# Hybrid attention / HGRN2 / mixture-of-experts layer on one core: two small loads moved to ScalarE's DMA queue, and unread products on TensorE around the first row transposes

## The chip, the cores and the metric

One core of a Trainium2 chip runs the whole layer as one program. The metric is the device time of one execution in microseconds (us), as the median of several runs. TensorE is called PE below, VectorE DVE, ScalarE ACT, GpSimd POOL and SyncE SP, as in the profile.

## What is computed

The reference is one layer over 16 meta tokens and 1024 tokens of width 1024. Cut to what matters here:

```python
h = concatenate([zeros, meta_tokens, x])              # rows of width 1024
a = rmsnorm(h, g_mix)                                 # x * rsqrt(mean(x^2) + eps) * g_mix
proj = a @ w_in                                       # 1024 -> 3584
# stick-breaking attention on 8 heads of 64, HGRN2 recurrence on 4 heads of 128,
# the latter with lower bounds lb = softmax(lb_logits) for its forget gate
h = h + mixed @ w_out
m = rmsnorm(h, g_ffn)
h = h + hierarchical_moe(m)                           # 4 groups x 8 experts, 2 experts per token
out = rmsnorm(h, g_final)
```

The change touches only the way from `x`, `meta_tokens`, `g_mix` and `lb_logits` to the first columns of `proj`.

## The kernel before, in words

**Stages.** The input rows are normed, transposed and split into a high and a low part (`aH`, `aL`, 1040 columns of tokens). Then four rounds follow, in each of which projections, the HGRN2 recurrence and stick-breaking attention run interleaved by `merge`; then the output projection and the router (up to about 750 us), then the 32 experts (up to about 1337 us), then the last norm. Every projection is three products per 128 rows of the contraction (`whi*aH`, `whi*aL`, `wlo*aH`, lines 203 to 205).

**The head of the program.** `head_project` for head 0 (lines 518 to 549) does the input norm as it goes. `load_rows(i)` (line 143) loads row block `i`: block -1 is the 16 meta tokens, blocks 0 to 7 are 128 tokens each; below they are called block -1, block 0 and so on. `norm_rows(i)` (lines 146 to 162) squares a block on ACT with a sum (line 152), makes the factor on DVE (line 100) and POOL (line 101), multiplies block, factor and `gm` on DVE into `xn` (line 154), transposes `xn` on PE in two halves of four (line 158), copies each half to `aH` on ACT (line 160) and subtracts on DVE into `aL` (line 161). `gm` is `g_mix` spread over the 128 partitions; its load stands between those of blocks 0 and 1 on SP's queue (line 519). `load_block` (line 189) loads a block of `w_in` into `wraw`, and `split_block(nc.gpsimd)` splits it on ACT (`whi`, line 195) and POOL (`wlo`, line 197); the first two blocks are the forget columns and the input columns of head 0. The blocks -1, 0 and 1 are normed first, then the two weight blocks are split, then block 2 is normed, then `project_chunk` makes the first 272 columns (`START[0]`: blocks -1, 0 and 1) of the forget projection, and so on alternately.

**The small load.** `lbt` holds `lb_logits` on 8 partitions. It is loaded on SP's queue at line 458, transposed at line 460, copied on DVE at line 462, and used in the evacuation of the forget projection (`ev_f`, lines 500 and 501). At line 529 the same load stands a second time.

**Order.** Each engine runs its instructions in the order in which the framework's scheduler placed them when the program was built; it places an instruction of an engine when its inputs are ready by the scheduler's own estimate, the earlier in the program text first. Instructions of different engines wait for each other by semaphores. The PSUM tag `tr` has two buffers, so the third transpose group waits for the DVE subtraction that reads the first.

**The unread products.** `warm(n)` (lines 815 to 822) multiplies the identity by itself `n` times into a PSUM bank of tag `o` that nobody reads, each product placed behind the one before. Before the change it is used only at the end of the router stage.

Of the kernel before, what the change touches and what calls it, by code (L numbers as in the profile page):

```python
# [18 lines left out]
P = 128  # L19
# [4 lines left out]
D = 1024  # L24
# [4 lines left out]
def bcast(ap, n):  # L29
    return bass.AP(tensor=ap.tensor, offset=ap.offset, ap=[[0, P], [1, n]])  # L30
# [3 lines left out]
def kernel(  # L34
# [21 lines left out]
    nc = tc.nc  # L56
# [14 lines left out]
    def behind(first, then):  # L71

        tc.add_manual_dep(then.ins, first.ins.name, mybir.DependencyInfo(mybir.DependencyClass.NoSync, mybir.DependencyReason.SCHED_ONLY), reason="order")

    def bank(tag):
        return psum.tile([P, 512], F32, name=tag, tag=tag)

    def bank4(tag):
        return bank(tag).rearrange("p (a b) -> p a b", b=P)


    ones = const.tile([P, P], F32, name="ones")
    nc.vector.memset(ones, 1.0)
# [5 lines left out]
    nc.vector.memset(small[:, 1:17], -0.5)  # L89
    zero, mhalf = small[:, 0:1], small[:, 1:17]  # L90
    nc.scalar.activation(small[:, 17:18], zero, AF.Sigmoid)

    def mixed_rows(i, n):

# [41 lines left out]

    gm = att.tile([P, NT + 1, 4, 64], F32, name="gm", tag="av", bufs=1).rearrange("p a b c -> p (a b c)")[:, :D]

    def load_rows(i):

        n = M if i < 0 else P
        xt = att.tile([P, W], F32, name="xt", tag=("beta1", "keep")[i % 2], bufs=2)[:n, :D]
        nc.sync.dma_start(xt, meta_tokens if i < 0 else x2[P * i:P * i + P])
        return xt

    def norm_rows(i, xt):

        n = M if i < 0 else P
        c0 = 0 if i < 0 else M + P * i
        ss = att.tile([P, 1], F32, name="xss")[:n]  # L150
        xn = att.tile([P, W], F32, name="xn", tag=("kh", "kl")[i % 2])[:n, :D]
        nc.scalar.activation(xn, xt, AF.Square, accum_out=ss)
        r = rstd_of(att, ss, 1, D, "rx")[:n]
        nc.vector.scalar_tensor_tensor(xn, xt, r, gm[:n], op0=ALU.mult, op1=ALU.mult)
        for h in range(2):
            pt = bank4("tr")
            for k in range(4):
                nc.tensor.transpose(pt[:, k, :n], xn[:, (4 * h + k) * P:(4 * h + k + 1) * P], ident[:n, :n])
            hi = aH[:, 4 * h:4 * h + 4, c0:c0 + n]
            nc.scalar.activation(hi, pt[:, :, :n], AF.Copy)  # L160
            done = nc.vector.tensor_sub(aL[:, 4 * h:4 * h + 4, c0:c0 + n], pt[:, :, :n], hi.bitcast(F32))  # L161
        return done

    def merge(*streams, until=None):

# [289 lines left out]


    lbt = mc.tile([8, P], F32, name="lbt")
    nc.sync.dma_start(lbt, lb_logits.rearrange("l (h d) -> (l h) d", d=P))
    lbp = bank("tr")
    nc.tensor.transpose(lbp[:, :8], lbt, ident[:8, :8])  # L460
    lbs = mc.tile([P, 4, 4], F32, name="lbs")
# [31 lines left out]
    def head_project(hd, Q2, F, kR, V):  # L493
# [19 lines left out]
        if hd > 0:  # L513
            yield from project(1536 + P * hd, REAL, ev_q)
            yield from project(2048 + P * hd, FULL, ev_f)
            yield from project(2560 + P * hd, FULL, ev_i)
        else:
            xs = {i: load_rows(i) for i in (-1, 0)}
            nc.sync.dma_start(gm, bcast(g_mix, D))
            for i in (1, 2):  # L520
                xs[i] = load_rows(i)
                load_block()
            for i in (-1, 0, 1):
                norm_rows(i, xs.pop(i))
                xs[i + 4] = load_rows(i + 4)
            split_block(nc.gpsimd)
            split_block(nc.gpsimd)
            (_, fh, fl), (_, ih, il) = halves.pop(0), halves.pop(0)
            nc.sync.dma_start(lbt, lb_logits.rearrange("l (h d) -> (l h) d", d=P))
            norm_rows(2, xs.pop(2))  # L530
            xs[6] = load_rows(6)
            yield from project_chunk(fh, fl, *START[0], ev_f)
            norm_rows(3, xs.pop(3))
            xs[7] = load_rows(7)
            yield from project_chunk(ih, il, *START[0], ev_i)
            norm_rows(4, xs.pop(4))
            load_block()
            yield from project_chunk(fh, fl, *START[1], ev_f)
            norm_rows(5, xs.pop(5))
            norm_rows(6, xs.pop(6))  # L540
            yield from project_chunk(ih, il, *START[1], ev_i)
            last = norm_rows(7, xs.pop(7))
            make_masks(last)
            nc.sync.dma_start(sbg, bcast(sb_gain, 512))
            nc.sync.dma_start(hgg, bcast(hg_gain, 512))
            yield from project_chunk(fh, fl, *START[2], ev_f)
            split_block()
            yield from project_chunk(ih, il, *START[2], ev_i)
            yield from project(1536, REAL, ev_q)
# [260 lines left out]
    def load_until(n):  # L810
        while len(pieces) < min(n, 6 * NE):
            e, part = divmod(len(pieces), 6)
            pieces.append(load_piece(slice(e, e + 1), part, len(pieces)))

    def warm(n, first=None):

        w = bank("o")[:, :P]
        for _ in range(n):
            mm = nc.tensor.matmul(w, lhsT=ident, rhs=ident, start=True, stop=True)
            if first is not None:  # L820
                behind(first, mm)
            first = mm

    def route(i, rp, r):

# [275 lines left out]
    turned = []  # L1101
# [244 lines left out]
```

## Time and profile before

| | us |
|---|---|
| median of 3 runs | 1359.17 |
| lowest and highest of the 3 | 1356.43 and 1359.87 |
| profiled execution, its own time | 1358.34 |
| its span, from first to last instruction | 1356.7 |
| PE busy | 1279.8 (94% of the span) |
| DVE busy | 1064.8 (78%) |
| ACT busy | 840.9 (62%) |
| POOL busy | 292.7 (22%) |

The rows further below come from the profiled execution. A row of the timeline has the start and the duration in us, the engine, the line, the operation, output and inputs with their shapes, how many instructions are merged into the row, and in square brackets the idle time of the engine before it and what ended that. SPq is SP's DMA queue: the duration is that of issuing, not of the transfer. [...] In the first stretch of the trace the granted clock is recorded as 1.00 throughout, also where the products take as long as at 0.50 elsewhere; there the durations are read.

### The profile page before, as it was taken

To read this page: it belongs to the slowest core of one execution; us is meant where nothing else is said; L and a number is where in the kernel's file an instruction comes from. 1 tells how busy PE (TensorE), PEld (TensorE's weight loads), DVE (VectorE), ACT (ScalarE), POOL (GpSimd) and SP (SyncE) were. 2 spreads that over 40 slices of the span, in tenths; PEclk is the share of its full clock that TensorE was granted. 3 is DMA by queue.
4 is the path that set the end of the run, shared out by engine and by line. 5 is a ranking of instruction groups with operands and counts; after the bars stand their busy time and mean duration, and the time that the engine had idled before them with its cause. 6 is when DMAs were issued, how large, how long until landed. Compare 5 with 4: busy or idle time off the path is not lost.

```text
span 1356.7 us, 19397 instructions
## 1 busy us (share of the span) xinstructions
PE 1279.8 (94%) x6872; PEld 1001.8 (74%) x6873; DVE 1064.8 (78%) x1677; ACT 840.9 (62%) x1374; POOL 292.7 (22%) x373
## 2 busy tenths in 40 slices
PE   6999889998999899999999999999999999999993
PEld 5888788877888788777888666666666666666661
DVE  5384887478756877699667888888898898898885
ACT  5333654266334643555223888888888888888884
POOL 3202340034103420252111111111111111111114
PEclk9999999999999999999999999999999999999996
DMA  6111001110011010175587699999999999999916
GB/s 204 46 33 47 21 24 36 39 44 20 24 31 48 24 36 21 53 239 176 198 297 254 233 400 406 398 376 409 361 374 399 361 402 374 371 407 366 359 40 264
DMA packets 84307, 278.65 MB, mean 205 GB/s; under 512 B 12806, under 2 KB 45598, under 8 KB 59632
## 3 DMA queue, kind: packets, MB, share of 16 engines
q1 hardware_dynamic: 70048, 243.53, 46.8%
q0 software_dynamic: 14016, 33.33, 8.3%
q8 instruction: 55, 0.90, 0.3%
q10 hardware_dynamic: 144, 0.52, 0.1%
q14 instruction: 44, 0.36, 0.1%
HBM read 258.59 MB, written 35.52 MB: 217 GB/s over the span
## 4 chain that ended last, share of the span: by engine, by line
issue 38%; PE 31%; DVE 11%; POOL 9%; DMA 6%; ACT 3%; POOLq 0%; SPq 0%; ACTq 0%; DVEq 0%
PE pj L205 6%; PE pj L204 6%; PE pj L203 5%; DVE keep L331 4%; POOL out_dram L1139 3%; POOL xg L1086 3%; DMA mrows<-mt 3%; DVE beta L336 2%; DMA out_dram<-y,idx 2%; PE o L382 2%; PE pj L776 1%; PE z L608 1%; POOL keep L323 1%; PE pj L775 1%; PE tr L355 1%
## 5 line engine op out<-in xcount | busy, mean ns | idle before, releaser
L1124 DVE TENSOR_TENSOR wl<-w,wh 128x1024 fp32r<-128x1024 f32 x384 | 457.1, 1220 | 62.2 <-ACT wh L1118 60.7
L1118 ACT ACTIVATE wh<-w 128x1024 fp32r<-128x1024 f32 x384 | 402.4, 1057 | 73.1 <-PE pj L1148 22.6
L203 PE MATMUL pj<-aH,whi 128*128 128x346 f32 (+4 forms) x576 | 208.8, 363 | 0.9 <-ACT aH L160 0.5
L204 PE MATMUL pj<-aL,whi 128*128 128x346 f32 (+4 forms) x576 | 203.1, 353 | 1.1 <-DVE aL L161 1.0
L205 PE MATMUL pj<-aH,wlo 128*128 128x346 f32 (+4 forms) x576 | 202.4, 351 | 0.0
L203 PEld LDWEIGHTS pj<-aH,whi 128*128 128x128 f32 x576 | 110.2, 192 | 8.2 <-ACT aH L160 1.2
L204 PEld LDWEIGHTS pj<-aL,whi 128*128 128x128 f32 x576 | 110.0, 191 | 7.7 <-DVE aL L161 1.7
L205 PEld LDWEIGHTS pj<-aH,wlo 128*128 128x128 f32 x576 | 109.9, 191 | 7.3
L1086 POOL DMA_INDIRECT xg<-mrows,idx x32 | 44.3, 1384 | 293.5 <-PE tr L1095 286.8
L1147 PE MATMUL o<-wl,hH 128*96 128x512 f32 x256 | 104.3, 407 | 0.8 <-DVE wl L1124 0.8
L1147 PE MATMUL pj<-wl,emH 128*96 128x512 f32 x256 | 103.9, 406 | 0.2 <-DVE wl L1124 0.2
L1146 PE MATMUL pj<-wh,emH 128*96 128x512 f32 x256 | 103.7, 405 | 0.3 <-ACT emH L1108 0.3
L1146 PE MATMUL o<-wh,hH 128*96 128x512 f32 x256 | 102.0, 398 | 1.7 <-ACT hH L1194 1.7
L1146 PE MATMUL z<-wh,emH 128*96 128x512 f32 x256 | 103.0, 402 | 0.0
L331 DVE TENSOR_TENSOR_SCAN keep<-keep,small 128x144 f32<-128x144 f32 (+3 forms) x64 | 90.9, 1421 | 12.9 <-POOL keep L323 12.1
L1148 PE MATMUL o<-wh,hL 128*96 128x512 f32 x256 | 101.0, 395 | 0.0
L1147 PE MATMUL z<-wl,emH 128*96 128x512 f32 x256 | 101.0, 394 | 0.0
L1148 PE MATMUL pj<-wh,emL 128*96 128x512 f32 x256 | 100.5, 393 | 0.4 <-DVE emL L1109 0.4
L1148 PE MATMUL z<-wh,emL 128*96 128x512 f32 x256 | 100.2, 392 | 0.0
L1139 POOL DMA_INDIRECT out_dram<-y,idx x31 | 49.1, 1583 | 183.5 <-ACT y L1204 183.5
L358 ACT ACTIVATE wH<-tr 128x512 fp32r<-128x512 f32 (+1 forms) x80 | 44.6, 558 | 56.6 <-PE tr L355 55.9
L195 ACT ACTIVATE whi<-wraw 128x1024 fp32r<-128x1024 f32 x28 | 29.6, 1058 | 74.9 <-PE pj L204 52.6
(285 smaller groups left out, 2586.4 us busy)
## 6 DMA issues: line engine op xcount, KB each, us to landing
w<-in_w_expert_gate_dram SPq DMA_DIRECT2D x64, 1024.0 KB, 8.5
w<-in_w_expert_up_dram SPq DMA_DIRECT2D x64, 1024.0 KB, 8.8
w<-in_w_expert_down_dram SPq DMA_DIRECT2D x64, 1024.0 KB, 7.9
wraw<-in_w_in_dram SPq DMA_DIRECT2D x28, 512.0 KB, 3.9
out_dram<-ht POOLq DMA_DIRECT2D x11, 512.0 KB, 3.7
xt<-in_x_dram SPq DMA_DIRECT2D x8, 512.0 KB, 4.6
wraw<-in_w_out_dram SPq DMA_DIRECT2D x8, 512.0 KB, 5.3
mxt<-mixed SPq DMA_DIRECT2D x16, 256.0 KB, 4.7
```

What stands on the lines that cost most here:

```text
L203: nc.tensor.matmul(ps[:, :n], lhsT=hi[:, k], rhs=aH[:, k, c0:c0 + n], start=k == 0, stop=False)
L204: nc.tensor.matmul(ps[:, :n], lhsT=hi[:, k], rhs=aL[:, k, c0:c0 + n], start=False, stop=False)
L205: nc.tensor.matmul(ps[:, :n], lhsT=lo[:, k], rhs=aH[:, k, c0:c0 + n], start=False, stop=k == KD - 1)
L331: nc.vector.tensor_tensor_scan(kr, kr, zero.to_broadcast([P, S]), 1.0, op0=ALU.mult, op1=ALU.add)
L358: nc.scalar.activation(hi[:, :n], pt[:, :n], AF.Copy)
L1086: nc.gpsimd.indirect_dma_start(out=dst, out_offset=None, in_=src, in_offset=bass.IndirectOffsetOnAxis(ap=ix, axis=0), bounds_check=T - 1, ...
L1118: nc.scalar.activation(wh, w, AF.Copy)
L1124: nc.vector.tensor_sub(wl, w, wh.bitcast(F32))
L1139: nc.gpsimd.indirect_dma_start(out=out2, out_offset=bass.IndirectOffsetOnAxis(ap=ix, axis=0), in_=y, in_offset=None, bounds_check=T - 1, o ...
L1146: nc.tensor.matmul(ps, lhsT=hi, rhs=wh[:, u], start=k + u == 0, stop=False)
L1147: nc.tensor.matmul(ps, lhsT=hi, rhs=wl[:, u], start=False, stop=False)
L1148: nc.tensor.matmul(ps, lhsT=lo, rhs=wh[:, u], start=False, stop=k + u == last)
```

## The change

`warm` is defined at the top of the kernel instead of before `route`. Twenty unread products stand right after the identity is made. The loads of `gm` and of `lbt` are issued from ACT's queue: that of `gm` where the tile is allocated, ahead of every row load in the text, and that of `lbt` at its old place in the text. The load of `gm` between the row loads is gone, and so is the second load of `lbt`. `norm_rows` can return its last transpose instead of its last subtraction, and two unread products are placed behind the last transpose of the blocks -1, 0, 1 and 2. The unread products are fp32, 128x128 by 128x128.

```diff
+    def warm(n, first=None):
+        w = bank("o")[:, :P]
+        for _ in range(n):
+            mm = nc.tensor.matmul(w, lhsT=ident, rhs=ident, start=True, stop=True)
+            if first is not None:
+                behind(first, mm)
+            first = mm
...
     nc.scalar.activation(small[:, 17:18], zero, AF.Sigmoid)
+
+    warm(20)
...
     gm = att.tile([P, NT + 1, 4, 64], F32, name="gm", tag="av", bufs=1).rearrange("p a b c -> p (a b c)")[:, :D]
+    nc.scalar.dma_start(gm, bcast(g_mix, D))
...
-    def norm_rows(i, xt):
+    def norm_rows(i, xt, turned=False):
...
-                nc.tensor.transpose(pt[:, k, :n], xn[:, (4 * h + k) * P:(4 * h + k + 1) * P], ident[:n, :n])
+                mm = nc.tensor.transpose(pt[:, k, :n], xn[:, (4 * h + k) * P:(4 * h + k + 1) * P], ident[:n, :n])
...
-        return done
+        return mm if turned else done
...
-    nc.sync.dma_start(lbt, lb_logits.rearrange("l (h d) -> (l h) d", d=P))
+    nc.scalar.dma_start(lbt, lb_logits.rearrange("l (h d) -> (l h) d", d=P))
...
             xs = {i: load_rows(i) for i in (-1, 0)}
-            nc.sync.dma_start(gm, bcast(g_mix, D))
...
             for i in (-1, 0, 1):
-                norm_rows(i, xs.pop(i))
+                warm(2, norm_rows(i, xs.pop(i), True))
                 xs[i + 4] = load_rows(i + 4)
...
-            nc.sync.dma_start(lbt, lb_logits.rearrange("l (h d) -> (l h) d", d=P))
-            norm_rows(2, xs.pop(2))
+            warm(2, norm_rows(2, xs.pop(2), True))
...
-    def warm(n, first=None):
```

## Rows read from the trace of the kernel before

**Rows 1.** The windows view of the expert stage: length, then busy time and instructions of PE, PE's weight loads, DVE, ACT and POOL, granted clock, DMA share, GB/s.

```profile
760.00:1320.00 560.00, 559.79 (x2615) 383.01 (x2614) 500.29 (x498) 470.94 (x560) 89.62 (x61) 1.00 0.93 361
```

**Rows 2.** The chain of work that ended last, in order of time, cut to the first 32 us (start us, us, what).

```profile
3.07 7.72 DMA wraw<-in_w_in_dram
10.81 1.07 ACT whi L195
11.95 2.75 POOL wlo L197
...
15.16 0.55 POOL rx L101
...
15.74 1.15 DVE xn L154
```

**Rows 3.** The timeline of the first 30 us, SP's queue alone: issues of loads.

```profile
0.83 0.40 SPq L458 DMA_DIRECT2D lbt<-in_lb_logits_dram  x1
1.29 0.33 SPq L143 DMA_DIRECT2D xt<-in_meta_tokens_dram  x1
...
2.12 0.43 SPq L519 DMA_DIRECT2D gm<-in_g_mix_dram  x1
2.59 0.43 SPq L143 DMA_DIRECT2D xt<-in_x_dram  x1
3.07 0.57 SPq L189 DMA_DIRECT2D wraw<-in_w_in_dram  x1
```

**Rows 4.** The windows view of the first 8 us in steps of 1 us, two of them; the last number is GB/s.

```profile
3.00:4.00 1.00, 0.00 (x0) 0.00 (x0) 0.00 (x0) 0.66 (x1) 0.00 (x0) 1.00 0.78 205
...
7.00:8.00 1.00, 0.00 (x0) 0.00 (x0) 0.30 (x3) 0.00 (x0) 0.57 (x1) 1.00 0.99 395
```

**Rows 5.** The timeline of all engines, 0 to 32 us: the identity, ACT's first work, the small load's transpose and copy, block 0's factor, block -1's and block 3's `xn`, and the second `wlo`.

```profile
0.83 1.28 ACT L91 ACT_TABLE_LOAD   x1 [0.70 <-PEq L1332]
...
1.17 0.34 POOL L85 TENSOR_SCALAR_AFFINE_SELECT ident<-ones 128x128 f32<-128x128 f32 x1
...
2.39 0.24 PE L460 MATMUL tr<-ident,lbt 8*128 8x8 f32 x1 [2.39 <-DMA lbt<-in_lb_logits_dram]
...
6.92 0.15 DVE L100 TENSOR_SCALAR rx<-xss 128x1 f32<-128x1 f32 x1 [2.26 <-ACT xn L152]
6.99 0.16 DVE L462 COPY lbs<-tr 128x8 f32<-128x8 f32 x1
...
7.84 1.27 DVE L154 SCALAR_TENSOR_TENSOR xn<-xt,rx,gm 16x1024 f32<-16x1024 f32 x1 [0.69 <-POOL rx L101]
...
16.41 2.85 POOL L197 TENSOR_TENSOR wlo<-wraw,whi 128x1024 fp32r<-128x1024 f32 x1 [0.70 <-ACT whi L195]
...
19.79 1.29 DVE L154 SCALAR_TENSOR_TENSOR xn<-xt,rx,gm 128x1024 f32<-128x1024 f32 x1 [1.50 <-POOL rx L101]
```

**Rows 6.** The timeline of PE alone, 9 to 24 us: transposes of blocks -1, 0 and 2, then the products of the forget projection's first chunk. From 18.45 to 21.72 eleven products are listed, from 22.22 to 23.35 ten.

```profile
9.17 1.03 PE L158 MATMUL tr<-ident,xn 16*128 16x16 f32 x8 [6.54 <-DVE xn L154]
10.82 1.97 PE L158 MATMUL tr<-ident,xn 128*128 128x128 f32 x8 [0.62 <-DVE aL L161]
...
17.68 1.12 PE L158 MATMUL tr<-ident,xn 128*128 128x128 f32 x4 [0.70 <-DVE aL L161]
18.45 0.57 PE L204 MATMUL pj<-aL,whi 128*128 128x272 f32 x1
...
19.05 1.05 PE L158 MATMUL tr<-ident,xn 128*128 128x128 f32 x4
...
20.36 0.43 PE L205 MATMUL pj<-aH,wlo 128*128 128x272 f32 x1
...
21.72 0.40 PE L205 MATMUL pj<-aH,wlo 128*128 128x272 f32 x1
...
22.22 0.29 PE L205 MATMUL pj<-aH,wlo 128*128 128x272 f32 x1
...
23.35 0.29 PE L205 MATMUL pj<-aH,wlo 128*128 128x272 f32 x1
```

**Rows 7.** The timeline of all engines, 23 to 31 us: block 3's transposes, the `xn` of blocks 5 and 6, and the first product of the second chunk that reads `aL`.

```profile
23.48 1.04 PE L158 MATMUL tr<-ident,xn 128*128 128x128 f32 x8
...
26.96 2.48 DVE L154 SCALAR_TENSOR_TENSOR xn<-xt,rx,gm 128x1024 f32<-128x1024 f32 x2 [0.40 <-POOL rx L101]
...
30.10 0.44 PE L204 MATMUL pj<-aL,whi 128*128 128x384 f32 x1 [0.95 <-DVE aL L161]
```

**Rows 8.** The timeline of PE, 746 to 753 us: the fourteen unread products of the old `warm(14)`, as 28 instructions.

```profile
749.77 3.37 PE L819 MATMUL o<-ident 128*128 128x128 f32 x28
```

**Rows 9.** The windows view in steps of 10 us, the three stretches between 60 and 740 us in which the granted clock (third number from the end) is not 1.00.

```profile
190.00:200.00 10.00, 8.24 (x48) 8.04 (x48) 9.59 (x20) 2.36 (x6) 4.12 (x4) 0.83 0.00 0
...
480.00:490.00 10.00, 8.12 (x55) 7.39 (x53) 9.72 (x12) 5.83 (x15) 2.63 (x5) 0.98 0.16 46
490.00:500.00 10.00, 10.00 (x64) 9.51 (x64) 6.33 (x18) 3.78 (x8) 2.22 (x2) 0.85 0.05 15
```

**Rows 10.** The windows view in steps of 1 us: before the first of these falls, and around 1329 us.

```profile
194.00:195.00 1.00, 0.00 (x0) 0.00 (x0) 1.00 (x3) 0.00 (x0) 0.00 (x0) 1.00 0.00 0
...
1327.00:1328.00 1.00, 0.48 (x4) 0.30 (x4) 1.00 (x1) 0.37 (x1) 0.00 (x0) 1.00 1.09 414
...
1330.00:1331.00 1.00, 1.00 (x3) 0.56 (x3) 1.00 (x1) 0.45 (x3) 0.72 (x1) 0.50 1.07 336
```

More of the change, by code (lines that the diff above doesn't have):

```diff
@@ L813, in load_until @@
             pieces.append(load_piece(slice(e, e + 1), part, len(pieces)))
-    def warm(n, first=None):
[L817 to L822, printed above, removed]
     def route(i, rp, r):
```

## The prediction, as put on record

> **What bounds the kernel now.** I read the page first, then the windows, then the chain of waits of the first 32 us, and last the timeline of the engines there. The profiled execution took 1358.34 us for a span of 1356.7. Nearly all of that is TensorE: in the expert stage PE is busy 559.79 of 560 us [rows 1]. Nothing downstream runs against an outside clock, so what the head of the program gives up moves the rest earlier by as much. The change can therefore be read in the first 30 us.
>
> There the chain of waits goes through the first weight block, not through the norm: the load of `wraw` is issued at 3.07 and lands 7.72 us later, ACT splits it at 10.81, POOL makes `wlo` until about 15.1, and only then does POOL come to block 2's factor at 15.16 and DVE to its `xn` at 15.74 [rows 2]. The rows of block -1 have their own earlier wait, `xn` at 7.84 [rows 5], but this one doesn't end last. From 17.68 on PE has work without pause: block 2's transposes, then the first chunk of the forget projection [rows 6]. The reader should see two speeds in rows 6: products of 272 columns follow each other every (21.72 - 20.36) / 6 = 0.227 us, and from about 21.9 on every (23.35 - 22.22) / 9 = 0.126 us. [...] The same pair shows in eight transposes: 1.97 us slow [rows 6], 1.04 fast [rows 7]. So the head pays twice: it waits for a weight block, and then does its first dense work at the low clock.
>
> **The change part by part.**
>
> *Loads moved off SP's queue.* The issues of `lbt` (0.83 to 1.29) and `gm` (2.12 to 2.59) leave the queue ahead of `wraw`'s [rows 3]: 0.46 + 0.47 = 0.93 us less before it is issued. The bytes ahead of it are the same, `gm`'s included, so the landing gains between 0 (if the engines that move bytes are the limit) and 0.93. They moved 205 GB/s from 3 to 4 us and 395 from 7 to 8 [rows 4], so the early part isn't full; I take 0.8. The split on ACT and POOL, block 2's factor and its `xn` move with it. The second `lbt` load stood on SP's queue behind three row loads, where nothing waited for it: 0. ACT issues the two loads instead; at SP's prices [rows 3] that is 0.9 us, ahead of its table load [rows 5] or behind it. At worst the squares of the first block start 0.9 later, which isn't on the chain either: 0. An earlier `gm` brings block -1's `xn` forward by at most 0.7 us (DVE is free from 7.15, starts at 7.84 [rows 5]), which isn't on the chain: 0.
>
> *Twenty unread products.* Fourteen show as 28 instructions in 3.37 us, (3.37 - 0.28) / 27 = 0.115 us each [rows 8], fast. Slow, I take the spacing of slow transposes, (1.97 - 0.43) / 7 = 0.22 [rows 6]. Forty instructions from about 1.55, when the identity is there [rows 5], end at 1.55 + 4.6 = 6.2 if all were fast and 1.55 + 8.8 = 10.4 if all were slow. I assume that the clock is low at first and rises on the way, as it did during the eleven products of rows 6, and take the middle, about 8.2. PE's next real job came at 9.17 [rows 6]: hidden. One wait is new: `lbt`'s transpose (line 460, at 2.39 before) now sits behind the twenty, and DVE's copy of it (line 462) stands in DVE's order right before block -1's `xn` [rows 5]. By 8.2 + 0.24 + 0.2 that `xn` would start at about 8.6 instead of 7.84, 0.8 late; blocks -1 and 0 get 0.9 + 0.4 back from faster transposes: 0, if the clock is up.
>
> *Two products behind each of four blocks.* Four instructions, 0.46 us fast, 0.88 slow. Behind blocks -1, 0 and 1 PE waits anyway (0.62 before block 0's transposes [rows 6], and longer once these are faster): 0. Behind block 2 PE is dense: +0.46.
>
> *The clock.* If it is still high at the first dense work, block 2's transposes take 1.04 instead of 1.12 + 1.05 = 2.17 (1.13 less), and eleven slow products [rows 6] save 11 x (0.227 - 0.126) = 1.1.
>
> *Sum.* -0.8 - 1.13 - 1.1 + 0.46 = -2.6 us at block 3's transposes (23.48 before). Are these ready then? They need block 3's `xn`, done at 19.79 + 1.29 = 21.08 [rows 5], which hangs on the second `wlo` on POOL (16.41 + 2.85) and moves with the weight loads: 20.3, against the 20.9 that PE then reaches. So that is late next, and it caps the gain at about 3.3. Behind it the way from 23.48 to the second chunk's product at 30.10 [rows 7] runs over DVE, with PE waiting 0.95 us, and moves as a whole.
>
> *What the trace does not price.* A shift of everything by 2 or 3 us changes where PE's pauses fall. PE stood still from 194 to 195 us [rows 10], and the granted clock fell after it: a mean of 0.83 over 10 us is 0.17 x 10 / 0.5 = 3.4 us at half rate, a loss of about 1.7 us; two rounds later it fell once more, by 0.02 + 0.15 [rows 9]. One such fall may come or go: -1.7 to +1.7, taken as 0, since as much speaks for either sign. The runs shown lie 3.44 us apart.
>
> **The rivals.**
>
> *The clock is low again at the first dense work.* Between the twenty products and the first chunk PE does transposes with pauses, and only six unread products. For it: from 9.17 to 17.68 PE ran mostly transposes, and those of block 2 were as slow as those of block 0 [rows 6]; near 1327 four transposes between two pauses weren't enough, and the next products ran at 0.50 [rows 10]. Against it: the pauses here would be near 1 us, shorter than the full stop at 194. Then the two clock terms vanish, the products behind block 2 cost 0.88, and -0.8 + 0.88 leaves about 1358.4: no change. [...]
>
> *More than the sum.* If the first chunk's products no longer alternate with block 2's transposes, the cap of 3.3 is reached, and with one fall of the clock avoided 1358.34 - 3.3 - 1.7 = 1353.3.
>
> *Slower: the new wait on DVE.* If the clock doesn't rise during the twenty products, they end at 10.4; `lbt`'s transpose and copy end at 10.8, and block -1's `xn` starts at 10.9, 3.1 us late, with block 0's and block 1's in DVE's order behind it. With 0.88 for the slow products behind block 2 that is 1358.34 + 4.0 = 1362.3. It decides from the point where the twenty end later than about 7.84 + 1.3 - 0.44 = 8.7: up to there the faster transposes pay the delay back. For it: the order on DVE [rows 5]. Against it: eleven slow products were enough for a rise in rows 6, and the scheduler may place the copy later.
>
> **How the numbers follow.** The sum is made against 1358.34; the median of the three runs is 1359.17, and the mean of all four times is 1358.45. 1358.45 - 2.6 = 1355.9 is the forecast. Chances: forecast 0.50, low clock again 0.26, more than the sum 0.14, slower 0.10. The range leaves out most of the slower rival and the end of the best one: 1352.8 to 1360.0, which holds the no-change rival with the spread of the runs. 0.3% of 1359.17 is 4.1 us, about what a measurement of this kernel can tell from no change. Faster by more than that means below 1355.1: the best rival and about a third of the forecast's chance, 0.31. Slower by more means above 1363.2: half of the slower rival, 0.06. The rest, 0.63, lies within.
>
> **What would show it.** In the new profile `wraw`'s issue stands near 2.1 and its split near 10.0; the twenty products end near 8.2, with their last ones 0.115 us apart; block 2's transposes start near 16.9 and take about 1.04; the first chunk's products are 0.126 apart from the first; block 3's transposes start near 20.9. Wrong would be: products 0.227 apart again after 17 us, block -1's `xn` after 9 us, or a head that is 2.6 us shorter with the same end.

## The result, and the profile after

The change made the kernel slower: a median of 1366.51 us (1365.11 to 1367.69, 6 runs) against 1359.52 us of the kernel before beside it, a ratio of 1.0056 [1.0043, 1.0069]. The profiled execution took 1366.9 us for a span of 1365.0, 8.3 us longer than the span of before.

All of it is lost in the head, and the places to compare are those of [rows 5 to 7]. The timeline of the kernel after, 0 to 40 us (start us, us, then engine, line, operation and what ended the idle time before it):

```profile
1.52 6.35 PE L85 MATMUL o<-ident 128*128 128x128 f32 x40 [1.52 <-POOL ident L94]
...
2.21 0.48 SPq L202 DMA_DIRECT2D wraw<-in_w_in_dram  x1
...
6.93 1.06 ACT L165 ACTIVATE xn<-xt 128x1024 f32<-128x1024 f32 x1 [1.54 <-DMA xt<-in_x_dram]
7.80 0.22 PE L473 MATMUL tr<-ident,lbt 8*128 8x8 f32 x1
...
8.23 1.27 DVE L167 SCALAR_TENSOR_TENSOR xn<-xt,rx,gm 16x1024 f32<-16x1024 f32 x1
...
9.55 0.41 PE L171 MATMUL tr<-ident,xn 16*128 16x16 f32 x4 [1.53 <-DVE xn L167]
...
10.01 1.06 ACT L208 ACTIVATE whi<-wraw 128x1024 fp32r<-128x1024 f32 x1 [0.55 <-DMA wraw<-in_w_in_dram]
...
16.05 2.33 POOL L210 TENSOR_TENSOR wlo<-wraw,whi 128x1024 fp32r<-128x1024 f32 x1
16.11 3.36 DVE L167 SCALAR_TENSOR_TENSOR xn<-xt,rx,gm 128x1024 f32<-128x1024 f32 x1 [0.72 <-POOL rx L112]
...
19.39 0.15 DVE L475 COPY lbs<-tr 128x8 f32<-128x8 f32 x1
...
19.59 0.61 PE L171 MATMUL tr<-ident,xn 16*128 16x16 f32 x4 [9.62 <-DVE lbs L475]
...
21.14 1.91 PE L171 MATMUL tr<-ident,xn 128*128 128x128 f32 x8
...
27.61 0.66 PE L171 MATMUL tr<-ident,xn 128*128 128x128 f32 x4 [0.95 <-DVE aL L174]
...
28.36 0.60 PE L171 MATMUL tr<-ident,xn 128*128 128x128 f32 x4
...
28.80 0.61 PE L85 MATMUL o<-ident 128*128 128x128 f32 x4
...
31.90 1.04 PE L171 MATMUL tr<-ident,xn 128*128 128x128 f32 x8
...
37.77 0.44 PE L217 MATMUL pj<-aL,whi 128*128 128x384 f32 x1 [0.20 <-DVE aL L174]
```

Read it from the bottom. The second chunk's product starts at 37.77, 7.67 us later than in [rows 7], and block 3's transposes at 31.90, 8.42 later. Block 0's transposes start at 21.14 in place of 10.82 [rows 6]. Above that stands the row that matters: PE has half of block -1's transposes done by 9.96, and then waits 9.62 us for DVE's copy of `lbt`'s transpose, which holds one of the two `tr` buffers until it is copied. In [rows 5] that copy ran at 6.99, ahead of block -1's `xn`. Now it runs at 19.39, behind the `xn` of blocks -1, 0, 1 and 2, although its input was ready at 8.02. (The last of these `xn`, at 16.11, takes 3.36 us beside POOL's `wlo` where the others take 1.28; the last section comes back to that.) DVE left the copy at its place behind these four for 11.37 us after its input was there; it is the order itself that is another one. The two `aL` of block -1 stand behind the copy as well (19.65 and 20.49).

What the change meant to do was done: `wraw` is issued at 2.21 instead of 3.07 [rows 3] and split at 10.01 instead of 10.81 [rows 2], and the twenty products end at 7.87. The clock rose and fell again: the forty instructions took 6.35 us, between the 4.6 and the 8.8 that the prediction worked out for all fast and all slow. The windows view of the kernel after in steps of 2 us (length, busy time of PE, its weight loads, DVE, ACT and POOL, granted TensorE clock third from the end, 1.00 being the full one):

```profile
12.00:14.00 2.00, 0.00 (x0) 0.00 (x0) 0.00 (x0) 1.45 (x3) 2.00 (x2) 0.50 1.05 396
...
24.00:26.00 2.00, 1.66 (x11) 1.66 (x12) 1.28 (x4) 1.23 (x4) 0.54 (x1) 0.65 0.72 120
26.00:28.00 2.00, 1.05 (x10) 0.83 (x9) 2.00 (x3) 1.61 (x4) 0.00 (x0) 1.00 1.00 366
```

PE stood idle from 9.96 on, the clock was at 0.50 from 12 to 24 us, and block 0's transposes took 1.91 us, as slow as the 1.97 of [rows 6]. From 26 us on it was at 1.00 again. So at the first dense work it was high: block 2's transposes take 0.66 + 0.60 us, where [rows 6] has 1.12 + 1.05, and the first chunk's products, where they run without a break, are 0.126 us apart.

In the two traces the sequences differ in the head alone: the last instruction that stands elsewhere is the 39th on DVE, the 35th on ACT and the 21st on POOL, and on PE nothing differs but the unread products. The delay of 7.67 us at the second chunk is still there as 8.3 at the end.

### The profile page after: what moved, and what is told of

The parts are those of the page before. It is cut to its first block, busy times and chain, and to the rows that moved or that the text cites. A ratio compares the mean times of both kernels' runs of the same rounds, so it can differ in the third digit from the quotient of the medians.

```text
span 1365.0 us, 19507 instructions
## 1 busy us (share of the span) xinstructions
PE 1287.1 (94%) x6928; PEld 1008.5 (74%) x6929; DVE 1067.2 (78%) x1677; ACT 841.0 (62%) x1374; POOL 290.2 (21%) x373
## 3 DMA queue, kind: packets, MB, share of 16 engines
q10 hardware_dynamic: 304, 1.05, 0.2%
## 4 chain that ended last, share of the span: by engine, by line
issue 38%; PE 30%; DVE 13%; POOL 9%; DMA 6%; ACT 3%; POOLq 0%; SPq 0%; ACTq 0%; DVEq 0%
PE pj L218 5%; PE pj L217 5%; PE pj L216 5%; DVE keep L344 4%; POOL out_dram L1141 3%; POOL xg L1088 3%; DMA mrows<-mt 3%; DVE beta L349 2%; DMA out_dram<-y,idx 2%; PE o L395 2%; PE pj L787 1%; PE pj L786 1%; PE tr L368 1%; PE pj L785 1%; POOL keep L336 1%
```

## The experiments

All ratios are to the kernel before, run beside the kernel in question, with a 95% interval. `behind(a, b)` is the kernel's own helper for an edge that only orders b after a when the program is built, and makes no wait on the chip; `after(a, b)` makes a real one.

### The parts alone (e1, e2), and the buffer (e3)

e1 is the kernel before with the twenty products, all loads at their old places; the second, unneeded load of `lb_logits` is left out.

```diff
+    warm(20)
...
-            nc.sync.dma_start(lbt, lb_logits.rearrange("l (h d) -> (l h) d", d=P))
```

> The kernel before with the twenty unread products alone: both small loads on SP's queue in their old places (the second load of lbt stays out), no products behind the blocks. Theory ORDER (the twenty products make the scheduler place the copy of lbt and block -1's subtractions on DVE behind the xn of four blocks; PE then stands still until about 19.6 us): slow like the changed kernel, ratio to before 1.003 to 1.006, block 0's transposes after 20 us. Theory LOADS (the loads on ACT's queue are late for the first blocks and the delay is theirs): ratio 1.000 within 0.002.

1368.6 us, 1.0072 [1.0053, 1.0092]. The twenty alone lose as much as the whole change: the products end at 9.01, the second half of block -1's transposes waits 9.31 us for the copy until 18.73, and block 3's stand at 32.73.

e2 is the whole change without any product in the head.

```diff
-    warm(20)
...
-                warm(2, norm_rows(i, xs.pop(i), True))
+                norm_rows(i, xs.pop(i))
```

> The changed kernel without any of the unread products at its head: the two loads on ACT's queue, the second load of lbt gone. ORDER: no standstill, ratio 0.998 to 1.001, block 0's transposes near 10 to 12 us. LOADS: ratio 1.003 or more, with block -1's and block 0's squares late.

1359.77 us, 1.0019 [1.0007, 1.0031]: the loads don't lose the 8 us, but they gain nothing either, and the ratio lies between the ranges of the two theories. The copy stands at its old place in DVE's order. Two rows of POOL in e2's timeline show another change of order:

```profile
11.21 2.37 POOL L209 TENSOR_TENSOR wlo<-wraw,whi 128x1024 fp32r<-128x1024 f32 x1 [1.17 <-ACT whi L207]
...
13.55 0.55 POOL L111 TENSOR_TENSOR rx<-rx,small 128x1 f32<-128x1 f32 x1
```

With the weight block earlier, its `wlo` was put ahead of block 1's factor on POOL; before, the factor came first. Block 1's `xn` runs at 14.13 instead of 11.69, and its transposes at 16.07.

e3 is the whole change with `lbt`'s transpose in a PSUM bank of its own, so that block -1's transposes need not wait for the copy.

```diff
-    lbp = bank("tr")
+    lbp = bank("z")
```

> The changed kernel with the transpose of lbt written into a PSUM bank of tag z instead of tr. Theory BUFFER (all of the loss is that lbt's transpose holds one of the two tr buffers until its late copy): loss gone, ratio 0.998 to 1.000, block 0's transposes near 11 us. ORDER: block -1's second half goes through near 10 us, but block 0's transposes still wait for block -1's subtractions, which stand behind the same xn on DVE: ratio 1.004 to 1.006, block 0's transposes after 19 us.

1363.67 us, 1.0044 [1.0028, 1.0061]. The timeline of e3:

```profile
9.51 0.67 PE L171 MATMUL tr<-ident,xn 16*128 16x16 f32 x8 [1.38 <-DVE xn L167]
...
19.31 0.15 DVE L475 COPY lbs<-z 128x8 f32<-128x8 f32 x1
19.58 0.35 DVE L174 TENSOR_TENSOR aL<-tr,aH 128x64 fp32r<-128x64 f32 x2
19.85 1.97 PE L171 MATMUL tr<-ident,xn 128*128 128x128 f32 x8 [9.03 <-DVE aL L174]
...
30.63 1.04 PE L171 MATMUL tr<-ident,xn 128*128 128x128 f32 x8
```

Block -1 is now transposed whole at 9.51, and block 0 waits instead, 9.03 us for `aL` of block -1, which is still behind the copy in DVE's order. Block 3's transposes come only 1.27 us earlier than in the kernel after. The shared bank is a small part; the order on DVE is the large one.

### The order taken away, and given alone (e4, e13, e14)

e4 is the whole change with edges that hold DVE's and ACT's old order in the head.

```diff
+        if i == -1:
+            behind(subs["copy"], st)
...
+        if i >= 1:
+            behind(subs[i - 2], st)
...
+            if col in (2048, 2560):
+                behind(highs[-1 if col == 2048 else 0], wh)
```

Here `st` is a block's `xn`, `subs[i]` its last `aL`, `highs[i]` its last `aH`, `wh` the split of a weight block on ACT.

> The whole change, with edges that only set the order and add no wait between engines: on DVE and ACT the head's instructions stand as in the kernel before (copy of lbt, xn of -1, xn of 0, subtractions of -1, then xn of 1 and so on; squares and weight splits behind the copies to aH as before). ORDER: the loss is gone, ratio 0.997 to 1.000, that is 1355 to 1359 us, and the prediction's clock term can be read. If the products or the loads themselves cost the time: ratio 1.003 or more. If the clock is low again at the first dense work: near 1.000, with products 0.227 us apart after 17 us; if it is high, near 0.998.

1360.05 us, 1.0014 [1.0002, 1.0026]. Block 0's transposes are back at 11.61 and take 1.09 us, fast, as the change intended. But block 1's wait until 19.07 for `aL`, since POOL's order is still the new one (`wlo` at 12.15 ahead of block 1's factor at 14.47) and block 1's `xn`, begun at 15.06 beside the second `wlo`, takes 3.35 us; block 3's stand at 27.12. Most of the loss is gone with the order on DVE and ACT alone, but not all of it, as the theory had it.

e13 is the other way round: the kernel before, no product added and no load moved, with edges that give DVE, ACT and POOL the order of the kernel after.

```diff
+        if i == 1:
+            subs["pow1"] = pows[-1]
+        if i == 2:
+            behind(st, subs["copy"])
...
+            if i == -1:
+                behind(subs["copy"], done)
...
+            if col == 2560:
+                behind(wh, subs["aH"])
+            if col == 2048:
+                behind(wl, subs["pow1"])
```

> The kernel before, with no product added and no load moved; order-only edges give DVE, ACT and POOL the sequence that they have in the kernel after up to block 2: the copy of lb's transposes behind xn(2), both aL of block -1 behind the copy, the first aH of block -1 behind the second whi, wlo of the first weight block ahead of the factor of block 1. Theory (the order of work is the cause): block -1's second half at 17 to 19.5 us, block 3's transposes at 29 to 32, 1362 to 1367 us, 0.3 to 0.6% slower than the kernel before. Rival (the twenty products, the pairs or the loads cost the time, and the order only went along): block 3's transposes at 23.5 to 25 us and the time within 0.1% of the kernel before.

1368.04 us, 1.0067 [1.0055, 1.0079]. The timeline of e13:

```profile
2.35 0.24 PE L475 MATMUL tr<-ident,lbt 8*128 8x8 f32 x1 [2.35 <-DMA lbt<-in_lb_logits_dram]
...
16.73 3.36 DVE L158 SCALAR_TENSOR_TENSOR xn<-xt,rx,gm 128x1024 f32<-128x1024 f32 x1 [0.72 <-POOL rx L103]
...
20.02 0.15 DVE L477 COPY lbs<-tr 128x8 f32<-128x8 f32 x1
...
20.22 2.50 PE L166 MATMUL tr<-ident,xn 16*128 16x16 f32 x12 [10.61 <-DVE lbs L477]
...
33.97 1.03 PE L166 MATMUL tr<-ident,xn 128*128 128x128 f32 x8
```

`lbt`'s transpose is there at 2.35, so its input does not hold the copy back; it runs at 20.02 because it stands there. ACT's and POOL's sequences in this trace are those of the kernel after, and DVE's too but for two pairs of neighbours. The order by itself costs what the whole change costs. Block 3's transposes come even later than I had expected (33.97 for 29 to 32), and the time is just above its range. Of the 2.07 us by which they are behind the kernel after, 0.63 stand already at the copy and at block 2's transposes (28.24). The rest comes behind these, where the clock is low without the pairs: block 2's transposes take 1.11 + 1.05 us, and the first chunk's products stay 0.227 us apart until 32.3.

e14 is the zero of the edges: the kernel before with those of e9 below, which hold its own order, and without the second load of `lb_logits`.

> The kernel before with the order-only edges of e9 to e12 and nothing of the change but that the second load of lb_logits is left out: every engine's sequence is that of the kernel before but for this load. It is the zero of e9 to e12. Theory: block 3's transposes at 23.3 to 23.7 us and the time within 0.1% of the kernel before. Rival (the edges cost time, so that what e9 to e12 still lose isn't the change's): 0.1% slower or more.

1357.56 us, 0.9988 [0.9979, 0.9998]; block 3's transposes at 24.04, the second chunk's product at 30.67. Its sequences on PE, DVE, ACT and POOL are those of the kernel before without exception. The 0.56 us at block 3 are the clock's: the first chunk's products stay 0.227 us apart until 23.1, and before until 21.7 [rows 6]. So where the clock rises during the first chunk, a place behind it is good to half a microsecond, and a time to about 0.1%: e14 is faster, with its head later. Edges of this sort cost nothing that shows here.

### A set whose order was not the old one (e5 to e8)

These four hold DVE, ACT, POOL and SP by edges, with block 2's norm placed between the two weight splits in the text: the whole change (e5), its loads (e6), its products (e7), and the whole without the twenty (e8).

```diff
+        if 1 <= i <= 5:
+            behind(subs[i - 2], st)
...
+                behind(facts[1 if col == 2048 else 2], wl)
```

`facts[i]` is a block's factor on POOL, `wl` the `wlo` of a weight block.

> The whole change, with order-only edges on DVE, ACT, POOL and SP, so that the head stands as in the kernel before up to block 4 (in e4 POOL still made the first wlo ahead of block 1's factor). Read at the start of block 3's transposes, 23.48 us before, 27.12 in e4. If the order on DVE and POOL is all of the loss: 21.5 to 23.5, ratio 0.998 to 1.000. Theory FIRST BLOCK (the early load of gm shares the DMA engines with block 0, whose square starts near 7.0 instead of 5.74, and the head hangs on that): 23 to 24.5, ratio near 1.000.

> The two loads on ACT's queue alone, no unread products at the head, same edges as e5. The prediction's term for the loads was -0.8 us: block 3's transposes at 22.7, ratio 0.9994. FIRST BLOCK: block 0's square at 7.0, block -1's xn at 8.3, block 3's transposes at 24.0 to 24.5, ratio 1.0003 to 1.001.

> The unread products alone (twenty and the pairs), both loads in their old places on SP's queue, same edges as e5. Block 0's square back at 5.7 us. If the clock stays high up to the first chunk: block 3's transposes at 21.0 to 22.0, ratio 0.998 to 0.999, products of the first chunk 0.126 us apart from the first on. If the clock falls again before it: 23 to 24.5, ratio near 1.000, and the first products 0.227 apart. If the copy of lbt waits for the twenty (PE done at 8.5) and delays block -1's xn to 8.9: a further 0.5 to 1.0 later.

> As e5 without the twenty products: the loads and the pairs behind the blocks, same edges. If the pairs alone can't raise the clock: slow transposes (1.97 us for eight) for blocks 0 and 1, block 3's transposes 0.5 to 1.5 us later than in e5, ratio 1.000 to 1.001. If the twenty buy nothing at the first chunk: the same as e5 within 0.3 us.

1360.8, 1361.15, 1363.11 and 1360.85 us; 1.0019 [1.0008, 1.0030], 1.0025 [1.0014, 1.0036], 1.0038 [1.0023, 1.0053] and 1.0023 [1.0013, 1.0032], all above what was expected. The head runs in the old order up to block 3 (transposes at 23.67 in e5, 25.17, 24.59 and 23.91 in the others), but the second chunk begins at 32.45 to 33.04 in all four. The timeline of e5:

```profile
28.14 1.53 DVE L171 SCALAR_TENSOR_TENSOR xn<-xt,rx,gm 128x1024 f32<-128x1024 f32 x1 [1.60 <-POOL rx L114]
29.59 1.28 DVE L189 TENSOR_TENSOR aL<-tr,aH 128x512 fp32r<-128x512 f32 x2
30.33 1.26 PE L185 MATMUL tr<-ident,xn 128*128 128x128 f32 x8 [2.51 <-DVE aL L189]
```

The `xn` at 28.14 is block 6's: the edges left it free, and it had overtaken block 5's and block 3's `aL`, for which block 4's transposes then wait 2.51 us. The times of these four say nothing fair about the parts of the change, and I don't use their ratios. They show the same mechanism a second time, made by my own edges.

Up to block 3 they can be read side by side. From the start of block 2's transposes to that of block 3's, the loads alone (e6) take 25.17 - 19.63 = 5.54 us, the loads with the pairs (e8) 23.91 - 19.53 = 4.38, and with the twenty as well (e5) 23.67 - 19.30 = 4.37. So the clock term of the prediction exists, with the pairs' own price it is worth 1.16 us in this stretch, and the twenty add nothing to it. The pairs don't always bring it: in e7, with twenty and pairs, the first four transposes of block 2 take 1.12 us, as without any product, and the stretch 24.59 - 19.03 = 5.56.

### The change in the old order, and the splits made to wait (e9 to e12)

e9 is e5 with the edges that were missing. DVE, ACT and POOL now run the sequence of the kernel before, instruction for instruction but for one 0.14 us factor.

```diff
-        if i == 0:
+        if i >= 0:
             behind(subs["st"], st)
...
+        if i == 5:
+            behind(subs["kR"], pows[-1])
```

> The whole change, with DVE, ACT and POOL held by order-only edges to the sequence of the kernel before, instruction for instruction (one 0.14 us rx on DVE sits one place earlier), so that block 6's xn no longer overtakes block 5's as it did in the four kernels of the set before. Theory (the loss is the order of work, first on DVE, and whatever else of the chain is lost is which of DVE's xn and POOL's wlo begins first): block -1's transposes at about 9.7 us, xn(1) again some 3.4 us long because wlo of the first weight block begins within 0.1 us of it, block 1's transposes at 16.0, block 3's at 23 to 24, the second chunk's L204 products at 30 to 31, and 1358 to 1360 us, within 0.2% of the kernel before. Rival (the products or the early loads cost time by themselves, through the clock or the DMA engines): the second chunk still begins at 32 us or later and its products are 0.5 us long at the lower clock; 1360 to 1362 us.

1360.66 us, 1.0015 [1.0004, 1.0026]. The timeline of e9:

```profile
12.23 2.35 POOL L231 TENSOR_TENSOR wlo<-wraw,whi 128x1024 fp32r<-128x1024 f32 x1
12.30 3.36 DVE L171 SCALAR_TENSOR_TENSOR xn<-xt,rx,gm 128x1024 f32<-128x1024 f32 x1 [0.74 <-POOL rx L114]
...
16.32 1.97 PE L191 MATMUL tr<-ident,xn 128*128 128x128 f32 x8 [3.35 <-DVE aL L195]
...
23.94 1.25 PE L191 MATMUL tr<-ident,xn 128*128 128x128 f32 x8
```

With the order whole, some 8 us become 2. The time lies a little above the theory's range and within the rival's (1360 to 1362), but the second chunk begins at 31.54 and its products take 0.34 us, not the rival's 0.5. What is left at block 1 is the pair at 12.23 and 12.30. In the kernel before, block 1's `xn` started at 11.69 and took 1.28 us, and it was `wlo` that took long, 3.26 us from 11.95. Here `wlo` is 0.07 us ahead, and `xn` takes 3.36.

e10 makes each of the two splits wait for the `xn` that it met.

```diff
-        facts[i] = pows[-1]
+        facts[i] = st
...
-                behind(facts[1 if col == 2048 else 2], wl)
+                after(facts[1 if col == 2048 else 2], wl)
```

> As the run before, and the two splits of the head on POOL wait for the xn that they ran into: wlo of the first weight block for xn(1), wlo of the second for xn(2). Theory (xn and wlo of this shape do not run side by side, and the one that begins second waits): xn(1) and xn(2) take 1.28 us each, xn(1) at about 12.0, wlo at about 13.3 for 2.4 us, block 1's transposes at about 14, block 3's at 21 to 22, so two microseconds ahead of the run before; the time 1356 to 1358.5 us, 0.0 to 0.2% under the kernel before. Rival (the long xn was waiting for something else, its data or its semaphore): xn(1) is still over 3 us long, and the time is that of the run before. Second rival (wlo is now late for the first chunk): its first product waits for wlo behind block 2's transposes and gives the two microseconds back.

1359.44 us, 1.0012 [1.0001, 1.0023]. The timeline of e10:

```profile
1.52 7.42 PE L85 MATMUL o<-ident 128*128 128x128 f32 x40 [1.52 <-POOL ident L94]
...
9.25 1.27 DVE L171 SCALAR_TENSOR_TENSOR xn<-xt,rx,gm 16x1024 f32<-16x1024 f32 x1
...
12.85 1.28 DVE L171 SCALAR_TENSOR_TENSOR xn<-xt,rx,gm 128x1024 f32<-128x1024 f32 x1 [0.73 <-POOL rx L114]
...
14.27 2.37 POOL L231 TENSOR_TENSOR wlo<-wraw,whi 128x1024 fp32r<-128x1024 f32 x1 [1.46 <-ACT aH L193]
14.79 1.25 PE L191 MATMUL tr<-ident,xn 128*128 128x128 f32 x8 [1.27 <-DVE aL L195]
...
17.17 1.28 DVE L171 SCALAR_TENSOR_TENSOR xn<-xt,rx,gm 128x1024 f32<-128x1024 f32 x1 [1.78 <-POOL rx L114]
...
21.50 1.28 DVE L171 SCALAR_TENSOR_TENSOR xn<-xt,rx,gm 128x1024 f32<-128x1024 f32 x1 [1.78 <-POOL rx L114]
...
23.44 1.25 PE L191 MATMUL tr<-ident,xn 128*128 128x128 f32 x8
```

The first theory held for the pair: `xn` of block 1 takes 1.28 us again, and block 1's transposes come 14.79 - 11.98 = 2.81 us behind block 0's, against 16.32 - 11.43 = 4.89 in e9. Its time and its place for block 3's transposes (21 to 22) did not come, since the 2.08 us don't last. 0.55 of them make up for the twenty products, which ended later in this execution (8.94 for 8.39). And the later `wlo` stands ahead of block 2's factor on POOL, so block 2's `xn` waits 1.78 us (0.72 in e9); at block 2's transposes (19.11 for 19.58) and at block 3's some 0.5 us of the lead is left. That is a third rival, on which I had not counted: the wait goes from DVE to POOL's queue.

e11 and e12 are the loads and the products by themselves, in the old order and with the two waits of e10.

> The loads of the change without any of its products, in the order of the kernel before, with the two splits waiting for xn(1) and xn(2). Theory: what is left is the loads by themselves: Square of block 0 about 1.1 us later than in the kernel before, block 0's transposes at 11.5 where before has 10.8, block 1's at 14.2, block 3's at 22.5 to 23.5; the time within 0.1% of the kernel before, 1357.5 to 1359.5 us. Rival (the loads' place gains the 0.8 us of the prediction's sum): block 3's transposes 0.8 us or more ahead of 23.48.

> The products of the change (the twenty and the pairs) with the loads at the places of the kernel before on SP's queue, in the order of the kernel before, with the two splits waiting for xn(1) and xn(2). Theory: block 0's transposes at the full clock at about 10.8, xn(1) at 11.7 for 1.28 us, block 1's transposes at about 13.5, block 3's at 21 to 22; the clock low again in part of the stretch between block 1 and the first chunk, since nothing but the pairs stands there; 1356 to 1358.5 us. Rival (the low clock that follows takes all of it back): block 3's transposes as before at 23.5, slow products in the second chunk, and 1358.5 to 1361 us.

e11: 1357.9 us, 1.0001 [0.9992, 1.0011]; block 3's transposes at 24.16. Its theory held for the time and up to block 1, and the rival's gain of 0.8 us did not come. e12: 1359.49 us, 1.0013 [1.0000, 1.0027]; block 3's transposes at 24.23 for 21 to 22. Its theory, a gain, failed. The clock fell ahead of the first chunk, as it had allowed for (0.83, 0.50 and 0.82 in the stretches of 2 us from 18 to 24), and the time is in the rival's range, though the second chunk's products are fast (0.34 us). The timeline of e11 has the reason for the loads:

```profile
6.96 1.06 ACT L168 ACTIVATE xn<-xt 128x1024 f32<-128x1024 f32 x1 [1.25 <-DMA xt<-in_x_dram]
...
8.28 1.26 DVE L170 SCALAR_TENSOR_TENSOR xn<-xt,rx,gm 16x1024 f32<-16x1024 f32 x1
...
10.01 1.28 DVE L170 SCALAR_TENSOR_TENSOR xn<-xt,rx,gm 128x1024 f32<-128x1024 f32 x1 [0.39 <-POOL rx L113]
```

`gm` is issued at 0.83 now, ahead of block 0's rows, and these land later: block 0's square on ACT starts at 6.96 where before had 5.74, and its `xn` at 10.01 where before had 9.12. It is so in every run: 6.85 to 7.05 in the ten traces with the loads moved, 5.66 to 6.44 in the six others. At block 1's `xn`, where the splits' waits don't yet count, the loads make e11 0.66 us late (12.35 for 11.69).

## Why the prediction was wrong

The forecast was 1355.9 us, the range ended at 1360.0, and 1366.51 came. The step that failed is the one in "Twenty unread products" that put the copy of `lbt`'s transpose "right before block -1's `xn`" and costed the new wait from there. It took the order of the kernel before as given, and of the one way in which it could change it wrote that "the scheduler may place the copy later", as an argument against a loss. The order did change, for the worse: the copy went behind four `xn`, with block -1's `aL` behind it. e1 shows that the twenty products are enough to bring this about, e13 that the order needs neither product nor load to cost 0.67%, and e9 that the change without it costs 0.15%. How the builder came to this order isn't shown; that `lbt`'s transpose stands behind forty instructions in PE's order, and so looks late to it, is the likely reason. None of the signs that the prediction named for the first 10 us could have caught it: `wraw`'s issue and split and the end of the twenty came as foretold, and block -1's `xn` ran at 8.23.

The rival "the new wait on DVE" had the right instruction and the wrong way to lose by it. It decides, as written, if the twenty end later than 8.7; they ended at 7.87, and the loss was there all the same. Its price of 4.0 us was half of the 8.4 at block 3's transposes.

The other terms, by what was measured:

- *Loads, -0.8.* `wraw`'s issue and split moved by 0.86 and 0.80 us, as costed. But the split can move so far only where ACT's order changes too. In the order of before it stands behind the copies of block -1 to `aH`, done at 10.62, and ACT is idle for only 0.19 us ahead of it:

```profile
10.31 0.31 ACT L160 ACTIVATE aH<-tr 128x64 fp32r<-128x64 f32 x2
...
10.81 1.06 ACT L195 ACTIVATE whi<-wraw 128x1024 fp32r<-128x1024 f32 x1 [0.19 <-DMA wraw<-in_w_in_dram]
```

So a chain that "goes through the first weight block, not through the norm" was too much said: the norm's copies are done only 0.19 us ahead of it, and with the loads moved but the order held the split starts at 10.79 (e11). A delay of the first squares was allowed for, through ACT's issuing, and put at 0; that `gm`'s load makes block 0's rows land later wasn't foreseen, and it is on the chain: 0.66 us late at block 1's `xn` in e11, not 0.8 early.

- *Twenty products, ending near 8.2, cost 0.* They ended at 7.87, 8.39 and 8.94 in the kernel after, e9 and e10. The step said that blocks -1 and 0 pay 0.8 us of delay back by faster transposes. In e10 block 0's transposes were fast, and most of the delay stayed: the `xn` of blocks -1, 1, 2 and 3 stand at 9.25, 12.85, 17.17 and 21.50, for 7.84, 11.69, 15.74 and 19.79 before, which is 1.41, 1.16, 1.43 and 1.71 late. In e12, without the loads, block -1's is 0.68 late (8.52) and block 1's 0.43 (12.12). So about 0.25 us is paid back up to block 1, not 1.3: the chain between blocks runs over DVE and POOL too. What comes behind block 1 in e10 and e12 holds the waits of the splits as well.
- *The clock, -1.13 and -1.1.* Right in the main. In the kernel after the clock was low (0.50) from 12 to 24 us, while PE waited, but high (1.00 from 26 us on) at the first dense work: block 2's transposes gain 2.17 - 1.26 = 0.91 us and the first chunk's products are 0.126 apart. The rival "low again" did not come true there; it did in e7, for half of block 2's transposes in e4, and for the first chunk in e12. The gain was lost in the 8.4 us of the order. In e10, with the order held, block 2's transposes take 0.66 + 0.60 us too, and block 3's stand at 23.44 for 23.48 [rows 7]: the gain on PE paid for the 1.4 us that the `xn` were late, and no more. Which work held the clock is shown only by comparison: in all seven traces without the pairs block 2's first four transposes take 1.11 or 1.12 us, with them 0.66 to 0.69 in seven of nine, and in e11, without any product, those of blocks 0 and 1 took 1.97.
- *Pairs, +0.46 behind block 2.* Right in size: in the kernel after the row is 0.61 us long with the end of its last product, and the next product starts 0.36 us behind its start (28.80 to 29.16).
- *The cap of 3.3.* By its own rows it is 23.48 - 20.28 = 3.2. It was never reached.
- *Nothing downstream runs against an outside clock.* Right, with the wrong sign: 7.67 us at the second chunk are 8.3 at the end.

What stays open: e9, e10 and e12 lie 0.12 to 0.15% above the kernel before, and e11 at 0; e14, their zero, lies 0.12% under it. The head doesn't explain the whole difference: in e12 the second chunk's product (30.90) is only 0.23 us behind that of e14. Leftovers of this size come from what the prediction took as 0, a fall of the clock more or less. Between 40 and 1320 us the windows view in steps of 10 us shows none in the profiled executions of e4 and e13, one in those of e2, e5 to e8, e10, e11 and e14, one of twice the length in e12, two in before, after, e3 and e9, and three in e1. From the second chunk's product to the end it takes 1324.1 and 1323.9 us in e4 and e13, 1326.1 in e14, 1327.3 in e12, 1326.6 and 1327.2 in before and after, 1328.3 in e9 and 1328.5 in e1, in line with the prediction's estimate of 1.7 us for a fall. The change's own loss is not of this kind, with two falls on either side. One execution of each kernel was profiled, so how many falls a median holds isn't known, and the sign of these 0.1% stays open. A version of the change that beats the kernel before was not found; e11, its loads with the two waits, is equal to it.

## What to carry to other kernels

Before you cost an added instruction, ask what the builder makes of the order of all others, and compare the sequences engine by engine, not only the rows that you moved; a sum over a fixed order is worth nothing if the order isn't fixed. Where a scheduler decides, hold the order that matters with edges (they cost nothing that showed, e14), check that they hold all of it (in e5 to e8 they didn't), and only then measure what the change does. And ask of each transfer or product moved forward which one it now meets: here an earlier load made the next rows land about 1 us later, and a split begun just ahead of the norm's product held it up for 2.1 us.

## What the runs showed of the hardware

*DVE's `xn` and POOL's `wlo` did not run side by side.* Both read two SBUF tensors. Alone they take 1.28 and 2.35 us. Where one began while the other ran, the one that started first ran at its own speed and the other ended about its own time after it: in e9 `wlo` runs from 12.23 to 14.58, and `xn`, begun at 12.30, ends at 15.66, 1.08 us behind it. In e14 it is the other way round; its timeline:

```profile
11.67 1.29 DVE L169 SCALAR_TENSOR_TENSOR xn<-xt,rx,gm 128x1024 f32<-128x1024 f32 x1 [0.73 <-POOL rx L113]
...
11.85 3.34 POOL L229 TENSOR_TENSOR wlo<-wraw,whi 128x1024 fp32r<-128x1024 f32 x1 [0.21 <-ACT whi L227]
```

Here `xn` ends at 12.96 and `wlo` at 15.19, 2.23 us behind it. Who started first decided 2.1 us on DVE (3.36 for 1.29). A small operation was hit too: in the kernel after, block 0's factor on POOL, begun 0.12 us behind block -1's `xn`, took 1.58 us where others take 0.54. DVE's `aL`, with one input in PSUM, was not: the timeline of the kernel before has two of them in their usual 1.28 us beside `wlo`.

```profile
11.95 3.26 POOL L197 TENSOR_TENSOR wlo<-wraw,whi 128x1024 fp32r<-128x1024 f32 x1 [0.29 <-ACT whi L195]
12.89 1.28 DVE L161 TENSOR_TENSOR aL<-tr,aH 128x512 fp32r<-128x512 f32 x2
```

What keeps `xn` and `wlo` apart was not shown. e10 shows the cure and its limit.

*The granted clock of the head reads 1.00 before it has ever risen.* The windows view of the kernel before shows 1.00 in each stretch up to 22 us, although block 0's transposes take 1.97 us and block 2's 2.17 there [rows 6]; in e13 it shows 1.00 throughout, with PE idle from 9.61 to 20.22. In the kernel after, where the twenty had run, the 0.50 of 12 to 24 us is recorded. In the head the durations of the instructions tell the clock, not that column. The scale for them stands further on in the kernel before, with products of 348 columns:

```profile
192.76 0.32 PE L203 MATMUL pj<-aH,whi 128*128 128x348 f32 x1
192.92 0.33 PE L204 MATMUL pj<-aL,whi 128*128 128x348 f32 x1
193.09 0.32 PE L205 MATMUL pj<-aH,wlo 128*128 128x348 f32 x1
...
198.11 0.49 PE L204 MATMUL pj<-aL,whi 128*128 128x348 f32 x1
198.40 0.49 PE L205 MATMUL pj<-aH,wlo 128*128 128x348 f32 x1
```

With 1.00 granted from 192 to 194 us the first three stand 0.165 us apart, with 0.50 from 197 to 199 the other two 0.29. That is 0.47 and 0.83 ns a column; the 0.126 and 0.227 us of the 272 columns in the head are 0.46 and 0.83.

*The same pause gave two outcomes.* In e9 and e10 PE waits 1.71 us for `aL` ahead of the second chunk. In e9 its products run on at full speed (0.34 us each); in e10 the windows view shows a fall:

```profile
30.00:32.00 2.00, 0.96 (x3) 0.97 (x4) 1.65 (x5) 0.00 (x0) 0.22 (x1) 0.77 0.00 0
32.00:34.00 2.00, 2.00 (x8) 2.00 (x7) 1.34 (x2) 0.00 (x0) 0.62 (x2) 0.50 0.00 0
```

The products there take 0.52 us, and block 5's transposes come 36.70 - 31.04 = 5.66 us behind the chunk's start, for 35.67 - 31.54 = 4.13 in e9: 1.5 us. What tells the two apart was not found.
